# Memory keys and values beside the gate projections, and value stores issued by ScalarE

## The chip, the cores and the metric

The kernel runs on one core of one Trainium2 chip. The metric is the device time of one execution in microseconds. Its engines are TensorE (PE in the profile; its weight loads are PEld), VectorE (DVE), ScalarE (ACT), GpSimd (POOL) and SyncE (SP), which here issues DMAs and computes nothing. Each engine executes its own list of instructions in order; semaphores order the lists among each other.

## The reference

A network of three blocks on a sequence of 1024 rows of 1024 numbers, in float32. The change lies in layer A, the first of the last two:

```python
mem_n = rms_norm_2(mem, mem_norm)                      # 256 memory tokens
hn = rms_norm_2(h, norm_pre[i])
k_m, v_m = ...  (mem_n @ w_mem_kv[i])                  # for both layers, 4 heads of 64
c_q, c_kv, k_r, q_m, gate = split_cols(hn @ w_in_a[j], [384, 256, 32, 256, 1024])
main = mla_mixer(c_q, c_kv, k_r, positions, ...)       # 12 heads; 64 plain and 32 rotary columns
mem_out = memory_attention(q_m, k_m, v_m)              # every row reads all memory tokens
y = concatenate([main, mem_out]) * silu(gate)
h = h + rms_norm_2(y @ w_out[i], norm_post[i])
```

`mla_mixer` norms the latents `c_q` and `c_kv`, projects them to queries, keys and values, applies the rotary embedding to 32 columns of each query and to the shared `k_r`, and runs causal softmax attention. Layer B is alike with plain keys and values and a forget gate.

## The kernel before

Every matmul is done three times with operands split into a high and a low part (`mm3`, lines 124 to 126). A weight tile is loaded raw by `split_w` (line 103), rounded by ScalarE to its high part (`w_hi`, 104), and GpSimd subtracts for the low part (`w_lo`, 105).

The stages run one after another: start, stick, then mix, mlp and `layer_a` together, then `attn_a`, then `layer_b`. Within a stage a framework reorders each engine's instructions by its own estimate of when they can run, with the order in which the code emits them as its base; what comes out is fixed before the run. `merge(a, na, b, nb)` runs two generators by turns, `na` steps of the one beside `nb` of the other, so that they are emitted interleaved.

`layer_a` emits, in this order:
- `mem_norm`: the 256 memory tokens as two tiles of 128 rows are loaded (line 1090, one buffer for both), normed (lines 143 to 169, with a square root on ScalarE for which it loads a function table), transposed by TensorE (178) and split into `mh` and `ml`.
- 14 gate projections of 24 matmuls with 512 columns each (`gate`, PSUM tile `ps_ad`), evacuated by ScalarE with Silu, for which a table is loaded too (1205), and stored (1206).
- tables for the rotary embedding, the shared rotary key, the memory queries, the two latents and their norms.
- the rotary columns of the queries, in three groups `g` of four heads: six projections (`ps_r`), multiplied on VectorE (1274, 1277), summed on GpSimd (1278), split into `rope_hi` and `rope_lo` on ScalarE and VectorE (112, 113), and stored to `qrd` with four DMAs per group (1283), each with 16 rows of four heads (256 KB). `rope_hi` and `rope_lo` of group 2 reuse the buffers of group 0.
- `mem()` merged with `values()`. `mem` has eight projections of 24 matmuls with 256 columns (`ps_mem`): for each of two layers and two pairs of heads one for keys and one for values, with weights of 512 KB each, copies between partitions within SBUF (360), transposes of the values (370), and stores to DRAM (`mkv`, 1118, 1119). `values` has 16 units of six matmuls with 384 columns (`ps_v`), each evacuated by ScalarE into one of four buffers `vt_a` (1307) and stored to `vd_a` (1310; 192 KB in runs of 512 bytes).

`attn_a` reloads what was stored: rotary queries by lines 1353 and 1354, values by 1319, memory keys and values by `load_mkv` (1126, 1127). Its pools take the memory that `layer_a` gave back, so its first key evacuation (332) waits for the last value store. The method `values` also makes the values of layer B (`vd_b`, with a table of forget gates beside it).

All DMAs are issued on SP in one list. Each DMA raises one of eight counters, taken in turn, and waits until the DMA that had the same counter before it has landed.

Of the kernel before, what the change touches and what calls it, by code (L numbers as in the profile page):

```python
# [28 lines left out]
class Net:  # L29
# [1148 lines left out]
    def layer_a(self):  # L1178

        nc, tc, a = self.nc, self.tc, self.a  # L1180
# [8 lines left out]
        with ExitStack() as s2:  # L1189
            d1 = s2.enter_context(tc.tile_pool(name="ad1", bufs=1))  # L1190
            d2 = s2.enter_context(tc.tile_pool(name="ad2", bufs=2))
            psm = s2.enter_context(tc.tile_pool(name="psad", bufs=6, space=PSUM))
            pst = s2.enter_context(tc.tile_pool(name="pstad", bufs=2, space=PSUM))
# [3 lines left out]
            def unit(w, h):  # L1197
                ps = psm.tile([P, H], F32, name="ps_ad", tag="ad")
                self.proj_T(ps, w, col, act, 8, h)
                return ps  # L1200

            def gate(m, w, h):
                ps = unit(w, h)
                g = d2.tile([P, H], F32, name="g_ad", tag="kr1")
                nc.scalar.activation(out=g, in_=ps, func=AF.Silu)
                nc.sync.dma_start(out=gT[m, :, h * H:h * H + H], in_=g)

            self.mem_norm(d1, pst)
            for m in range(0, 8, 2):
                ws = [self.split_w(a["w_a_gate"][m + j], 1024) for j in range(2)] if m else self.g01  # L1210
                for h in range(0 if m else 1, 2):
                    for j in range(2):
                        gate(m + j, ws[j], h)
            cos = d1.tile([P, S], F32, name="cos")
            sin = d1.tile([P, S], F32, name="sin")
            rc = d1.tile([P, 3], F32, name="rope_c")
# [4 lines left out]
            w = self.split_w(a["w_a_kr"], 1024)  # L1221
# [12 lines left out]
            for p in range(2):  # L1234
                T = {k: d1.tile([P, S], F32R, name=f"qm_{k}", tag=f"qm_{k}") for k in ("qa", "qb")}
                w = self.split_w(a["w_a_qm"][p], 1024)
# [28 lines left out]
            for g in range(3):  # L1265
                w = self.split_w(a["w_mla_r"][g], 384)
# [19 lines left out]

            vt = d1.tile([P, 4, 384], F32, name="vt_a", tag="xq")

            def values():
                for n in range(2):  # L1290
                    w = [self.split_w(a["w_mla_v"][n], 768)]
                    yield from self.values(self.vd_a[3 * n:3 * n + 3], w, 2, range(3, 5), psm, "ad", vt)

            self.merge(self.mem(psm, pst, d2), 8, values(), 16)

    def values(self, vd, ws, kp, kts, psm, tag, vt, more=0, use=None):


        n = 384 + more
        hi, lo = self.act_hi, self.act_lo  # L1300
        for t in range(NT):
            ts = slice(t * P, (t + 1) * P)
            ps = psm.tile([P, n], F32, name="ps_v", tag=tag)
            self.mm3(ps, [((hi[:, k, ts], lo[:, k, ts]), tuple(w[:, (j % kp) * n:(j % kp) * n + n] for w in ws[j // kp]))
                          for j, k in enumerate(kts)])
            v = vt[:, t % 4]
            self.nc.scalar.activation(out=v, in_=ps[:, :384], func=AF.Copy)
            if more:
                use(t, ps[:, 384:])
            self.nc.sync.dma_start(out=vd[:, :, t, :].rearrange("q p c -> p q c"),  # L1310
                                   in_=v.rearrange("p (q c) -> p q c", c=P))
            yield

# [86 lines left out]
    def fox_gates(self, st):  # L1400
# [26 lines left out]
        def early(psm):  # L1427
            units.append(values(psm, 0))
            for _ in range(6):
                next(units[0])  # L1430
# [193 lines left out]
```

## Time and profile before

| | |
|---|---|
| median of three runs | 2968.9 us |
| runs | 2968.9, 2965.43, 2971.95 us |
| the profiled execution | 2973.59 us, span 2971.8 us |
| mean granted clock of TensorE | 0.972 |
| TensorE busy | 2774.5 us, 93% of the span |
| ScalarE busy | 1218.9 us, 41% |
| bytes moved by DMA | 311.14 MB, mean 105 GB/s |

Times in the rows below are microseconds from the start of the span. "Idle" in a row is the time for which the engine stood still ahead of the instruction, and the name behind the arrow is what it waited for. A granted clock of 1.00 is 2.4 GHz, 0.50 is 1.2 GHz.

### The profile page before, as it was taken

Reading aid. Unit: us, or ns where it says so; the run is one execution under the profiler, and the core shown is the slowest. Engines: PE = TensorE matmul, PEld = TensorE weight load, DVE = VectorE, ACT = ScalarE, POOL = GpSimd, SP = SyncE. Lnnn points to the kernel's source line nnn. Section 1 sums busy time; section 2 is a strip of 40 time slices with the busy share of each in tenths; the row PEclk is TensorE's granted clock in tenths of the full one; section 3 lists DMA queues with packets and bytes.
Section 4 is the critical chain, followed back from the end, with each engine's and each line's share of the span. In section 5 each row is a group of like instructions: output and inputs, shape, how many; then the busy total and the mean of one; then the engine's idle time right before and its main releaser. Section 6 shows DMA issues by size and latency. Waiting matters only on the chain. (4 is left out here: it accounts for less than half of the span.)

```text
span 2971.8 us, 37779 instructions
## 1 busy us (share of the span) xinstructions
PE 2774.5 (93%) x13490; PEld 2312.0 (78%) x13490; DVE 1692.0 (57%) x3201; ACT 1218.9 (41%) x2368; POOL 995.9 (34%) x823
## 2 busy tenths in 40 slices
PE   7999999998999998999989899689989999999988
PEld 5888778877878887888867689677768978778867
DVE  6320288845387665666587435287872426666643
ACT  5111266642442222121144423377763535555543
POOL 4221111113345442223255212332324344455442
PEclk9999999998999999999989899799999999999999
DMA  5111211127323335323123322632344232222162
GB/s 206 50 44 63 75 56 55 61 70 263 109 77 122 108 106 193 108 90 109 43 82 144 116 87 71 184 116 92 112 142 168 99 112 65 72 72 73 49 234 93
DMA packets 130644, 311.14 MB, mean 105 GB/s; under 512 B 14796, under 2 KB 34892, under 8 KB 130456
## 3 DMA queue, kind: packets, MB, share of 16 engines
q1 hardware_dynamic: 130456, 308.72, 31.0%
q8 instruction: 107, 1.75, 0.2%
q14 instruction: 81, 0.66, 0.1%
HBM read 213.33 MB, written 85.38 MB: 101 GB/s over the span
## 5 line engine op out<-in xcount | busy, mean ns | idle before, releaser
L105 POOL TENSOR_TENSOR w_lo<-w_raw,w_hi 128x1024 fp32r<-128x1024 f32 (+5 forms) x220 | 452.8, 2067 | 1057.8 <-ACT w_hi L104 1055.6
L104 ACT ACTIVATE w_hi<-w_raw 128x1024 fp32r<-128x1024 f32 (+5 forms) x220 | 192.5, 886 | 407.2 <-PE ps L125 90.7
L124 PE MATMUL ps_m<-act_hi,w_hi 128*128 128x512 f32 x716 | 289.8, 405 | 28.6 <-ACT w_hi L104 11.6
L125 PE MATMUL ps_m<-act_lo,w_hi 128*128 128x512 f32 x716 | 283.9, 397 | 0.0
L126 PE MATMUL ps_m<-act_hi,w_lo 128*128 128x512 f32 x716 | 282.4, 396 | 0.0
L113 DVE TENSOR_TENSOR pl<-tp_at,ph 128x512 fp32r<-128x512 f32 (+3 forms) x416 | 222.8, 560 | 85.9 <-ACT ph L112 83.8
L112 ACT ACTIVATE ph<-tp_at 128x512 fp32r<-128x512 f32 (+3 forms) x416 | 196.8, 500 | 106.2 <-PE tp_at L299 95.8
L1017 DVE TENSOR_TENSOR acc<-ps_d,acc 128x512 f32<-128x512 f32 x240 | 161.9, 687 | 109.7 <-PE ps_d L126 109.7
L299 PE MATMUL tp_at<-ident,p 128*128 128x128 f32 x1280 | 204.2, 275 | 16.1 <-DVE pl L113 5.7
L254 ACT ACTIVATE p<-p,mx 128x256 f32<-128x256 f32 (+7 forms) x256 | 180.3, 706 | 81.9 <-DVE mx L243 50.3
L124 PE MATMUL ps_d<-w_hi,act_hi 128*128 128x512 f32 x512 | 202.4, 395 | 7.7 <-ACT act_hi L112 7.7
L125 PE MATMUL ps_d<-w_lo,act_hi 128*128 128x512 f32 x512 | 202.0, 395 | 0.0
L126 PE MATMUL ps_d<-w_hi,act_lo 128*128 128x512 f32 x512 | 199.4, 392 | 0.0
L299 PEld LDWEIGHTS tp_at<-ident,p 128*128 128x128 f32 x1280 | 152.1, 140 | 48.5 <-DVE pl L113 9.1
L124 PEld LDWEIGHTS ps_m<-act_hi,w_hi 128*128 128x128 f32 x716 | 136.8, 191 | 64.8 <-ACT w_hi L104 12.7
L751 PE MATMUL r_o<-w_hi,act_hi 128*128 128x512 f32 x384 | 151.1, 403 | 20.5 <-DVE ga L687 7.9
L126 PEld LDWEIGHTS ps_m<-act_hi,w_lo 128*128 128x128 f32 x716 | 136.0, 190 | 28.6
L125 PEld LDWEIGHTS ps_m<-act_lo,w_hi 128*128 128x128 f32 x716 | 136.9, 191 | 25.9
L291 PE MATMUL o_ps<-ph,v 128*128 128x512 f32 (+3 forms) x400 | 145.5, 364 | 8.5 <-ACT ph L112 4.3
L753 PE MATMUL r_o<-w_hi,act_lo 128*128 128x512 f32 x384 | 151.7, 396 | 0.0
L752 PE MATMUL r_o<-w_lo,act_hi 128*128 128x512 f32 x384 | 151.3, 396 | 0.0
L292 PE MATMUL o_ps<-pl,v 128*128 128x512 f32 (+3 forms) x400 | 146.7, 374 | 0.4 <-DVE pl L113 0.2
(389 smaller groups left out, 6938.1 us busy)
## 6 DMA issues: line engine op xcount, KB each, us to landing
w_raw<-in_w_in SPq DMA_DIRECT2D x40, 512.0 KB, 3.4
w_raw<-in_w_up SPq DMA_DIRECT2D x32, 512.0 KB, 3.9
f_rows_up<-f_out SPq DMA_DIRECT2D x32, 512.0 KB, 5.4
w_raw<-in_w_down SPq DMA_DIRECT2D x32, 512.0 KB, 4.4
f_raw<-f_rows_up SPq DMA_DIRECT2D x32, 512.0 KB, 3.8
xd<-x_o SPq DMA_DIRECT2D x16, 512.0 KB, 2.7
w_raw<-in_w_out SPq DMA_DIRECT2D x16, 512.0 KB, 8.6
x_o<-xd SPq DMA_DIRECT2D x16, 512.0 KB, 4.8
```

The source lines that it names most:

```text
L104: nc.scalar.activation(out=hi[:, sl], in_=raw, func=AF.Copy)
L105: nc.gpsimd.tensor_tensor(out=lo[:, sl], in0=raw, in1=hi[:, sl].bitcast(F32), op=ALU.subtract)
L112: nc.scalar.activation(out=hi, in_=src, func=AF.Copy)
L113: nc.vector.tensor_tensor(out=lo, in0=src, in1=hi.bitcast(F32), op=ALU.subtract)
L124: nc.tensor.matmul(out, lhsT=sh, rhs=mh, start=(i == 0), stop=False)
L125: nc.tensor.matmul(out, lhsT=sh, rhs=ml, start=False, stop=False)
L126: nc.tensor.matmul(out, lhsT=sl, rhs=mh, start=False, stop=(i == n - 1))
L254: nc.scalar.activation(out=p[:, :nk], in_=p[:, :nk], func=AF.Exp, scale=-1.0, bias=mx[:, 0:1], accum_out=it["sum"][:, j:j + 1])
L299: nc.tensor.transpose(tp[:, j * P:(j + 1) * P], it["p"][j][:, k * P:(k + 1) * P], self.ident)
L752: nc.tensor.matmul(r, lhsT=a, rhs=wl, start=False, stop=False)
L753: nc.tensor.matmul(r, lhsT=b, rhs=wh, start=False, stop=(k == 7))
L1017: nc.vector.tensor_tensor(out=acc[:, t, sl], in0=ps, in1=acc[:, t, sl], op=ALU.add)
```

## The change

The eight steps of `mem()` are emitted beside the 14 gate projections, right after `mem_norm`, and `values` runs alone behind the rotary columns. The store of each unit of values is issued by ScalarE, in layer A and in layer B; its place in the rotation of counters is shared with the DMAs that stay on SP.

```diff
--- before.py
+++ after.py
@@ -1206,11 +1206,16 @@
                 nc.sync.dma_start(out=gT[m, :, h * H:h * H + H], in_=g)
 
             self.mem_norm(d1, pst)
-            for m in range(0, 8, 2):
-                ws = [self.split_w(a["w_a_gate"][m + j], 1024) for j in range(2)] if m else self.g01
-                for h in range(0 if m else 1, 2):
-                    for j in range(2):
-                        gate(m + j, ws[j], h)
+
+            def gates():
+                for m in range(0, 8, 2):
+                    ws = [self.split_w(a["w_a_gate"][m + j], 1024) for j in range(2)] if m else self.g01
+                    for h in range(0 if m else 1, 2):
+                        for j in range(2):
+                            gate(m + j, ws[j], h)
+                            yield
+
+            self.merge(gates(), 14, self.mem(psm, pst, d2), 8)
             cos = d1.tile([P, S], F32, name="cos")
             sin = d1.tile([P, S], F32, name="sin")
             rc = d1.tile([P, 3], F32, name="rope_c")
@@ -1286,12 +1291,10 @@
 
             vt = d1.tile([P, 4, 384], F32, name="vt_a", tag="xq")
 
-            def values():
-                for n in range(2):
-                    w = [self.split_w(a["w_mla_v"][n], 768)]
-                    yield from self.values(self.vd_a[3 * n:3 * n + 3], w, 2, range(3, 5), psm, "ad", vt)
-
-            self.merge(self.mem(psm, pst, d2), 8, values(), 16)
+            for n in range(2):
+                w = [self.split_w(a["w_mla_v"][n], 768)]
+                for _ in self.values(self.vd_a[3 * n:3 * n + 3], w, 2, range(3, 5), psm, "ad", vt):
+                    pass
 
     def values(self, vd, ws, kp, kts, psm, tag, vt, more=0, use=None):
 
@@ -1307,7 +1310,7 @@
             self.nc.scalar.activation(out=v, in_=ps[:, :384], func=AF.Copy)
             if more:
                 use(t, ps[:, 384:])
-            self.nc.sync.dma_start(out=vd[:, :, t, :].rearrange("q p c -> p q c"),
+            self.nc.scalar.dma_start(out=vd[:, :, t, :].rearrange("q p c -> p q c"),
                                    in_=v.rearrange("p (q c) -> p q c", c=P))
             yield
 
```

What follows is in lines of the changed kernel where they differ by a few: evacuation of values 1310, their store 1313, rope stores 1288, loads of rotary queries 1356 and 1357.

TensorE at the head of the gate stage, `ps_ad` being a gate and `tp<-ident,xn_m` the transposes of the normed memory tokens. Before:

```order
L126 MATMUL ps_ad<-act_hi,w_lo 128x512
L125 MATMUL ps_ad<-act_lo,w_hi 128x512
L126 MATMUL ps_ad<-act_hi,w_lo 128x512
L178 MATMUL tp<-ident,xn_m 128x128 x8
L124 MATMUL ps_ad<-act_hi,w_hi 128x512
L125 MATMUL ps_ad<-act_lo,w_hi 128x512
L126 MATMUL ps_ad<-act_hi,w_lo 128x512
```

and now:

```order
L124 MATMUL ps_ad<-act_hi,w_hi 128x512
L125 MATMUL ps_ad<-act_lo,w_hi 128x512
L126 MATMUL ps_ad<-act_hi,w_lo 128x512
L178 MATMUL tp<-ident,xn_m 128x128 x16
L124 MATMUL ps_mem<-mh,w_hi 128x256
L124 MATMUL ps_ad<-act_hi,w_hi 128x512
L125 MATMUL ps_ad<-act_lo,w_hi 128x512
L126 MATMUL ps_ad<-act_hi,w_lo 128x512
```

Before, 58 gate matmuls stand between the first of them and the first eight transposes, and 47 between those and the other eight. Now 24 stand ahead of the first, and the sixteen stand in one row with the first memory matmul behind them.

SP in the stage of the values, from the first rope store. Before:

```order
L1283 DMA qrd<-rope_hi 4x16x1024 x2
L1283 DMA qrd<-rope_lo 4x16x1024 x2
L360 DMA m_ka<-m_ka 64x256
L360 DMA m_kb<-m_kb 64x256
L1310 DMA vd_a<-vt_a 128x3x128 x2
L1118 DMA mkv<-m_ka 128x256
L1118 DMA mkv<-m_kb 128x256
L1118 DMA mkv<-m_kl 128x256
L103 DMA w_raw<-in_w_mla_v 128x768
L103 DMA w_raw<-in_w_mem_kv 128x1024
L1283 DMA qrd<-rope_hi 4x16x1024 x2
L1283 DMA qrd<-rope_lo 4x16x1024 x2
```

and now:

```order
L1288 DMA qrd<-rope_hi 4x16x1024 x2
L1288 DMA qrd<-rope_lo 4x16x1024 x2
L103 DMA w_raw<-in_w_mla_k 128x256
L103 DMA w_raw<-in_w_mla_q 128x384
L1357 DMA act_hi<-qrd 32x1024
L1356 DMA act_hi<-qrd 64x1024
L1288 DMA qrd<-rope_hi 4x16x1024 x2
L1288 DMA qrd<-rope_lo 4x16x1024 x2
L1356 DMA act_hi<-qrd 64x1024
L1357 DMA act_hi<-qrd 32x1024
L1288 DMA qrd<-rope_hi 4x16x1024 x2
L1288 DMA qrd<-rope_lo 4x16x1024 x2
```

The memory copies, stores and weights are gone from between the rope stores, the value stores are too, and the loads of rotary queries (`act_hi<-qrd`) have moved up between the groups of stores: the load with 64 rows, ahead of group 1, reads what all four stores of group 0 wrote.

ScalarE there. Before:

```order
L1307 ACTIVATE vt_a<-ps_v 128x384
L112 ACTIVATE rope_hi<-rope_14272 128x512
L1307 ACTIVATE vt_a<-ps_v 128x384
L366 ACTIVATE vt<-ps_mem 128x256
L112 ACTIVATE rope_hi<-rope_14290 128x512
L1307 ACTIVATE vt_a<-ps_v 128x384
L112 ACTIVATE rope_hi<-rope_14320 128x512
L1307 ACTIVATE vt_a<-ps_v 128x384
L104 ACTIVATE w_hi<-w_raw 128x768
```

and now:

```order
L1310 ACTIVATE vt_a<-ps_v 128x384
L1313 DMA vd_a<-vt_a 128x3x128
L112 ACTIVATE rope_hi<-rope_14631 128x512
L1310 ACTIVATE vt_a<-ps_v 128x384 x2
L104 ACTIVATE w_hi<-w_raw 128x256
L1313 DMA vd_a<-vt_a 128x3x128 x2
L112 ACTIVATE rope_hi<-rope_14661 128x512
L1310 ACTIVATE vt_a<-ps_v 128x384 x2
L104 ACTIVATE w_hi<-w_raw 128x384
L1310 ACTIVATE vt_a<-ps_v 128x384
L1313 DMA vd_a<-vt_a 128x3x128 x2
L112 ACTIVATE rope_hi<-rope_14679 128x512
```

Each evacuation is now followed, at once or after one or two other instructions, by the store of its buffer on the same engine. By the rotation of counters the fifth store waits for the second `rope_hi` store of group 0 to have landed, the tenth for one of `rope_hi` of group 1, the eleventh and twelfth for those of `rope_lo` of group 1, the fifteenth for the second `rope_hi` store of group 2, and the sixteenth for the first `rope_lo` store of group 2.

## Rows read from the trace of the kernel before

**Rows 1.** The page: its first line, and the first line of its part 1 (busy time of each engine, share of the span, instructions).

```profile
span 2971.8 us, 37779 instructions
...
PE 2774.5 (93%) x13490; PEld 2312.0 (78%) x13490; DVE 1692.0 (57%) x3201; ACT 1218.9 (41%) x2368; POOL 995.9 (34%) x823
```

**Rows 2.** Windows: the stretch, its length, busy time and instructions of TensorE (PE), its weight load, VectorE, ScalarE and GpSimd, then granted clock, DMA share and GB/s. Two of the seven windows of 20 us from 1700 to 1840, which all read 20.00 for TensorE.

```profile
1700.00:1720.00 20.00, 20.00 (x90) 16.57 (x89) 19.52 (x21) 4.64 (x6) 5.69 (x2) 1.00 0.32 113
...
1820.00:1840.00 20.00, 20.00 (x171) 20.00 (x171) 13.41 (x51) 8.81 (x33) 2.40 (x1) 1.00 0.14 47
```

**Rows 3.** Timeline of TensorE: start, length, engine, line, operation, what it writes and reads, count, and in brackets the idle time before it and who ended it, at the head of the gate stage. tp<-xn_m are the transposes of the memory tokens.

```profile
1662.96 0.96 PE L124 MATMUL ps_ad<-act_hi,w_hi 128*128 128x512 f32 x3 [0.69 <-ACT act_hi L112]
...
1681.98 1.94 PE L178 MATMUL tp<-ident,xn_m 128*128 128x128 f32 x8 [5.07 <-issue]
...
1696.12 1.04 PE L178 MATMUL tp<-ident,xn_m 128*128 128x128 f32 x8
```

**Rows 4.** The same view of ScalarE (ACT), VectorE (DVE) and SP there: the chain that normalises the two tiles of memory tokens.

```profile
1674.68 1.06 ACT L163 ACTIVATE xn_m<-m 128x1024 f32<-128x1024 f32 x1 [6.02 <-DMA rope_c<-in_rope_const]
...
1675.85 1.28 ACT L145 ACT_TABLE_LOAD   x1
...
1686.09 1.06 ACT L163 ACTIVATE xn_m<-m 128x1024 f32<-128x1024 f32 x1 [1.54 <-DMA m<-in_mem]
...
1678.48 3.40 DVE L169 SCALAR_TENSOR_TENSOR xn_m<-m,rstd_y,g_mem 128x1024 f32<-128x1024 f32 x1 [0.22 <-DVE rstd_y L149]
...
1691.39 1.28 DVE L169 SCALAR_TENSOR_TENSOR xn_m<-m,rstd_y,g_mem 128x1024 f32<-128x1024 f32 x1
...
1681.94 0.33 SPq L1090 DMA_DIRECT2D m<-in_mem  x1
```

**Rows 5.** Windows of that stretch, columns as in rows 2.

```profile
1682.00:1684.00 2.00, 2.00 (x9) 2.00 (x10) 0.27 (x1) 0.64 (x2) 0.00 (x0) 0.50 0.44 94
...
1688.00:1690.00 2.00, 2.00 (x11) 1.65 (x10) 0.00 (x0) 1.98 (x3) 1.49 (x1) 1.00 0.11 42
```

**Rows 6.** Timeline of TensorE in the stage of the values: the first and last of 17 memory matmuls (ps_mem, 256 columns) in a row.

```profile
1923.81 0.28 PE L125 MATMUL ps_mem<-ml,w_hi 128*128 128x256 f32 x1
...
1925.73 0.28 PE L126 MATMUL ps_mem<-mh,w_lo 128*128 128x256 f32 x1
```

**Rows 7.** Groups of instructions between 1855 and 1945: line, engine, operation, shapes, count | busy us, mean ns | idle time before them and who ended it.

```profile
L124 PE MATMUL ps_mem<-mh,w_hi 128*128 128x256 f32 x64 | 19.8, 309 | 22.0 <-ACT w_hi L104 16.9 <-ACT vt_a L1307 5.0
...
L1307 ACT ACTIVATE vt_a<-ps_v 128x384 f32<-128x384 f32 x16 | 7.6, 486 | 26.2 <-DMA vd_a<-vt_a 24.6 <-PE ps_v L126 1.5
```

**Rows 8.** Timeline of SP, the queue of all DMAs: issues of the rope stores (each row stands for two stores) and of the last value store. The length is that of the issue.

```profile
1858.42 1.23 SPq L1283 DMA_DIRECT2D qrd<-rope_hi  x2
1860.67 2.77 SPq L1283 DMA_DIRECT2D qrd<-rope_lo  x2
...
1876.91 1.15 SPq L1283 DMA_DIRECT2D qrd<-rope_hi  x2
...
1893.06 1.18 SPq L1283 DMA_DIRECT2D qrd<-rope_hi  x2
...
1928.96 0.41 SPq L1310 DMA_DIRECT2D vd_a<-vt_a  x1
```

**Rows 9.** Timelines of ScalarE and VectorE: the instructions there that waited for a rope store (qrd) or a value store (vd_a) to land.

```profile
1869.51 0.63 ACT L112 ACTIVATE rope_hi<-rope 128x512 fp32r<-128x512 f32 x1 [2.61 <-DMA qrd<-rope_hi]
...
1893.66 1.06 ACT L1307 ACTIVATE vt_a<-ps_v 128x384 f32<-128x384 f32 x2 [8.99 <-DMA vd_a<-vt_a]
...
1909.63 0.49 ACT L1307 ACTIVATE vt_a<-ps_v 128x384 f32<-128x384 f32 x1 [12.60 <-DMA vd_a<-vt_a]
...
1874.45 0.69 DVE L113 TENSOR_TENSOR rope_lo<-rope,rope_hi 128x512 fp32r<-128x512 f32 x1 [4.77 <-DMA qrd<-rope_lo]
```

**Rows 10.** Windows in the stage of the values, columns as in rows 2.

```profile
1862.00:1864.00 2.00, 2.00 (x18) 2.00 (x17) 1.91 (x5) 0.84 (x2) 2.00 (x1) 1.00 0.25 66
1880.00:1882.00 2.00, 0.75 (x3) 0.75 (x4) 1.31 (x4) 1.53 (x5) 2.00 (x2) 0.50 0.25 74
1898.00:1900.00 2.00, 0.00 (x0) 0.00 (x0) 0.00 (x0) 0.00 (x0) 0.00 (x0) 0.50 0.26 93
1920.00:1925.00 5.00, 5.00 (x42) 5.00 (x41) 1.18 (x4) 1.26 (x4) 0.12 (x1) 1.00 1.09 333
```

**Rows 11.** Timelines of ScalarE and TensorE at the end of that stage: the first key evacuation of the attention and its first score matmul.

```profile
1931.35 0.59 ACT L332 ACTIVATE ka<-ps_m 64x512 fp32r<-64x512 f32 x1 [0.33 <-DMA vd_a<-vt_a]
...
1942.19 0.41 PE L221 MATMUL s_ps<-act_hi 128*128 128x256 f32 x1
```

**Rows 12.** The line of the value stores, in layer A and in layer B: count, then shortest, median and longest issue in ns, first and last start; the last row is the time from issue to landing in layer B.

```profile
L1310 SPq DMA_DIRECT2D vd_a<-vt_a x16: 384/641/1992, 1866.8 to 1929.0; - x16
...
L1310 SPq DMA_DIRECT2D vd_b<-vt_b x15: 359/360/377, 2335.3 to 2395.6; - x15
...
DMA to landing us min/median/max: 2.0/2.3/2.7
```

**Rows 13.** A window of the values of layer B, columns as in rows 2.

```profile
2355.00:2375.00 20.00, 20.00 (x120) 19.76 (x119) 3.30 (x8) 9.38 (x16) 3.65 (x2) 1.00 0.16 49
```

## The prediction

> **What bounds the kernel now.** The page comes first: TensorE is busy for 93% of a span of 2971.8 us [rows 1], so a change pays only where TensorE waits, and costs wherever it adds work to a stretch in which TensorE never waits. Then I read the two stretches the change touches, in windows and in the timeline of each engine.
>
> Stretch A, the gate projections and what follows, is saturated: from 1700 to 1840 every window of 20 us shows TensorE busy for all 20.00 at a granted clock of 1.00 [rows 2]. One hole lies at its head. TensorE has 58 gate matmuls in front of the first transpose of the normalised memory tokens; they run from 1662.96 to about 1676.9, and the transpose waits until 1681.98 [rows 3] for a chain of one token tile: ScalarE's xn_m at 1674.68, a table load, VectorE's xn_m from 1678.48 for 3.40 us. The second tile's load is issued only at 1681.94, when that releases its buffer, and its xn_m starts on ScalarE at 1686.09 [rows 4]. That costs nothing today: 47 more gate matmuls stand between the two groups of transposes. After the hole TensorE runs at half clock (0.50, then 1.00 from 1688) [rows 5].
>
> Stretch B, from 1855 to 1942, holds the memory tokens' projections and the values, and TensorE waits there: 22.0 us before its ps_mem groups, while ScalarE's value evacuations wait 24.6 us for the stores of their four buffers [rows 7]. What ends B is the landing of the last value store: ScalarE's first key evacuation of the attention ends its wait on vd_a at 1931.35, and the first scores start at 1942.19 [rows 11]. Before it, three groups of rope stores pace everything (four stores of 256 KB each). The first group is issued from 1858.42 [rows 8]; its first pair has landed at 1869.51 and its second at 1874.45 [rows 9], so a group takes 16.0 us. The value stores behind group two end their wait at 1893.66, those behind group three at 1909.63 [rows 9], 16.8 and 16.6 us after the groups' first issues at 1876.91 and 1893.06 [rows 8]. A window in which almost nothing else moves shows a DMA share of 0.25 or 0.26 at 66 to 93 GB/s [rows 10]: a fraction of the engines, fully taken.
>
> **The change part by part.** I count by when events happen, against 2973.59 us of the profiled run, which is 4.7 above the median of 2968.9.
>
> 1. Memory projections into A. 192 matmuls, 0.12 us apart (16 steps from 1923.81 to 1925.73 [rows 6]), are 23.0 us; with the value transposes, 23.5. A has no idle TensorE time to take them [rows 2], so all of what follows is later by that.
>
> 2. The head of A. The order now puts 24 gate matmuls before the transposes instead of 58, and nothing between the two groups. At the 0.23 us a matmul of today (13.9 us for 58 [rows 3]) and with 0.6 for transposes among them they end at about 1669.1. The first tile is ready at 1681.98 as now, since its chain hangs on ScalarE's 1674.68 [rows 4]: 12.9 us idle. The second: load issued at 1681.94, xn_m at 1686.09 for 1.06; from the end of the first xn_m (1675.74) to VectorE's start are 2.74 us with a table load of 1.28 inside, 1.46 without it, as the load is gone; then 1.28 for the other xn_m [rows 4]: ready at 1689.9. TensorE ends the first eight transposes at 1683.9 (1.94 us [rows 3]): 6.0 idle. Together 18.9 against 5.07 today: +13.8, and about +1 because the second eight run at half clock (1.94 instead of 1.04 [rows 3]): +14.8. Bounds: 13, if VectorE's first xn_m takes 1.28 instead of 3.40 and wins half of that; 18, as the gate evacuation and the table load now stand ahead of rstd_t (0.6 + 1.28), and the weights' half-clock spell may repeat.
>
> Rope, stores and values thus start 38.3 us later. On SP the memory stores and copies now lie between gate loads; A's DMA share is 0.14 to 0.32 [rows 2], so I take nothing for them.
>
> 3. Stretch B without the memory tokens. Start is the first rope store (1858.42 before, 1896.7 after). By SP's order each loads-from-qrd now stands ahead of the next group's stores and waits for the group before it: group two cannot be issued until group one landed, 16.0 + 0.5. Group three's first pair is issued once group two's first pair landed, so it queues behind group two without a gap. For groups two and three I take 13.5 us, 1.05 MB at 78 GB/s, the mean of the three rows [rows 10]. The value stores now wait on ScalarE. Every DMA waits until the one eight earlier in its rotation has landed, and by the order of both queues the last two value stores come behind group three's first pair and its third store: three quarters of a group, 10.1 us. Then the last store, 2.3 us, what the same store takes in layer B where little else moves [rows 12]. Sum 16.0 + 0.5 + 13.5 + 10.1 + 2.3 = 42.4, against 72.9 today (1858.42 to 1931.35): 30.5 back. Bounds: at the best rate, 93 GB/s [rows 10], a group takes 11.3, and a first group of 14 gives 36.3; at the 16.7 of group two, with 3 us for the last store, 48.7. ScalarE has time for it: 16 evacuations of 0.49 [rows 7] and 16 issues of 0.64 [rows 12] are 18 us. Behind a waiting store stand the next evacuation and rope_hi of the next group; the order puts rope_hi of group two behind the fifth store, which waits for a pair that lands 11 us in, still before the 16.5. TensorE needs 17 us for the values and waits anyway.
>
> The Trainium skill speaks here: page "DMA: Bandwidth & Descriptors", section "Why a DMA increments its semaphore by 16 and not by 1", has a copy run on the largest number of engines, up to 16, that divides the slowest dimension of both sides, which for four heads by sixteen rows is four. The share of about 0.25 [rows 10] agrees. Its specifications give about 27 GiB/s for an engine, so four would take an estimated 9 us for a group; the sum for B by that is 27.6, not 42.4, and the rows, where no window at that share passes 93 GB/s, speak against it.
>
> 4. Values of layer B by ScalarE. 16 issues of 0.36 us [rows 12] are 5.8 us on an engine that is busy 9.4 of 20 us at most beside a saturated TensorE [rows 13]: nothing, and 5.8 if that cover were gone.
>
> The sum: 23.5 + 14.8 - 30.5 = **+7.8 us**, 2981.4 for the profiled run and 2976.7 for the median: 2977. With all bounds on one side: 23.0 + 13 - 36.6 = -0.6 and 24 + 18 - 24.2 = +17.8.
>
> **The rivals.** First, forecast: slower by 2 to 18, chance 0.60.
>
> Second, rope groups at the best rate seen, 93 GB/s: B takes 33.6 (11.3 + 0.5 + 11.3 + 8.5 + 2.0), net -1.0, 2968. For it: the queue no longer carries memory stores and weights. Against: group one took 16.0 with little beside it [rows 8, 9, 10]. Chance 0.22.
>
> Third, faster: the rope stores need less than 9.4 us a group when nothing shares the queue. To show as faster, B must come down by 38.3 + 5.9 from 72.9, to 28.7 us; less 0.5 and 2.3 that is 25.9 for two groups and three quarters. At 8.5 us a group B takes 8.5 + 0.5 + 8.5 + 6.4 + 2.3 = 26.2, net -8.4, 2960. The point from which it decides is 9.4 us a group, 112 GB/s. For it: the same core moves 333 GB/s in another window of B [rows 10], and layer B's value stores land in 2.0 to 2.7 us [rows 12]. Against it: no row at that share is near it. By the 9 us that the Trainium skill's page gives for four engines, above, B takes 27.6 and the result is 7.0 faster, on this side of the point. Chance 0.15.
>
> Fourth, slower by 20: the value stores on ScalarE hold up rope_hi of groups two and three, so that the groups no longer touch, and B takes 16.0 + 16.7 + 2 + 16.6 + 3 = 54.3: 2973.6 + 19.7, 2989 for the median. For it: ScalarE executes in order and waits in front of each store. Against: only the fifth and ninth store stand before such a step. Chance 0.03; it is the far end of the first.
>
> **How the numbers follow.** A change of this kernel shows from about 0.2%, 5.9 us; three runs spread over 6.5. The predicted time is the first case's, 2977; its own range is 2970 to 2987. The whole range reaches to the third case at 2960 and to just under the fourth: 2960 to 2988. Slower by over 0.2% is some five sixths of the first and the fourth: 0.53. Within it: the rest of the first and nearly all of the second: 0.31. Faster: the third and a little of the second: 0.16.
>
> **What would show it.** At the head of A: idle before the transposes of xn_m of about 12.9 and 6.0 us instead of 5.07. Between 1690 and 1890: ps_mem groups without idle time, and the first rope store near 1897. In B: ScalarE's issue of value stores waiting on DMA qrd, group two issued some 16.5 us after group one, group three landing some 40 us after the first store, the key evacuation ending its wait on vd_a near 1939 and the first scores near 1950. The prediction is wrong if the rope groups land in under 9.4 us each, if TensorE finds other work at the head of A, or if the end of B hangs on something the last value store does not hold.

## The result, and the profile after

The changed kernel takes 2987.57 us (median of four runs, 2983.82 to 2990.25) against 2967.16 for the kernel before (four runs, the three listed above and one more): the ratio, which is estimated apart from these medians, is 1.0075, with a 95% interval of 1.0058 to 1.0092. It is slower by 0.75%, as forecast; the forecast was 2977, 8 us slower, and it is 20 us slower. Nothing of the 20 us is more work; the page still gives TensorE the same busy time, over a longer span (compare [rows 1]):

```profile
span 2986.9 us, 37758 instructions
...
PE 2775.1 (93%) x13490; PEld 2311.6 (77%) x13490; DVE 1683.0 (56%) x3201; ACT 1216.5 (41%) x2366; POOL 993.8 (33%) x823
```

The span grew by 15.1 us between the two profiled executions; the profiled execution of before was 6.4 us above the median of its runs and that of the changed kernel 1.1 above its own, and the 5.3 between them is the rest. I count in the two traces, and come back to the scatter at the end.

At the head of the gate stage, the timeline of TensorE (compare [rows 3]):

```profile
1663.46 0.50 PE L124 MATMUL ps_ad<-act_hi,w_hi 128*128 128x512 f32 x1 [0.69 <-ACT act_hi L112]
...
1680.18 1.94 PE L178 MATMUL tp<-ident,xn_m 128*128 128x128 f32 x8 [10.49 <-issue]
1688.15 1.94 PE L178 MATMUL tp<-ident,xn_m 128*128 128x128 f32 x8 [6.03 <-DVE xn_m L169]
```

and the chain that normalises the memory tokens, on ScalarE, VectorE and SP (compare [rows 4]):

```profile
1673.57 1.06 ACT L163 ACTIVATE xn_m<-m 128x1024 f32<-128x1024 f32 x1 [8.54 <-DMA rope_c<-in_rope_const]
...
1684.38 1.06 ACT L163 ACTIVATE xn_m<-m 128x1024 f32<-128x1024 f32 x1 [1.62 <-DMA m<-in_mem]
...
1678.80 1.28 DVE L169 SCALAR_TENSOR_TENSOR xn_m<-m,rstd_y,g_mem 128x1024 f32<-128x1024 f32 x1 [0.21 <-DVE rstd_y L149]
...
1686.72 1.28 DVE L169 SCALAR_TENSOR_TENSOR xn_m<-m,rstd_y,g_mem 128x1024 f32<-128x1024 f32 x1
...
1680.11 0.33 SPq L1090 DMA_DIRECT2D m<-in_mem  x1
```

The first transposes wait 10.49 us and the second 6.03, instead of 5.07 in all, and both groups run at half clock (1.94 us each). VectorE's first xn_m took 1.28 us where it took 3.40 before, so the first tile was ready 1.8 us sooner than forecast.

Behind the head the stage is as saturated as it was, with the memory projections inside, while in the stage of the values TensorE now works for 1.34 of 20 us (windows; columns as in [rows 2]):

```profile
1720.00:1740.00 20.00, 20.00 (x102) 17.00 (x101) 1.43 (x4) 6.83 (x11) 9.42 (x4) 1.00 0.49 167
1800.00:1820.00 20.00, 20.00 (x90) 16.54 (x89) 6.31 (x8) 5.88 (x10) 3.34 (x2) 1.00 0.31 109
1920.00:1940.00 20.00, 1.34 (x6) 1.01 (x6) 1.24 (x3) 3.57 (x7) 0.00 (x0) 0.58 0.52 158
```

The stage of the values, from SP's list (compare [rows 8]; a row stands for two stores, or for one load of rotary queries, act_hi):

```profile
1895.01 1.25 SPq L1288 DMA_DIRECT2D qrd<-rope_hi  x2
...
1912.57 0.51 SPq L1356 DMA_DIRECT2D act_hi<-qrd  x1
1913.14 1.11 SPq L1288 DMA_DIRECT2D qrd<-rope_hi  x2
...
1925.99 0.32 SPq L1357 DMA_DIRECT2D act_hi<-qrd  x1
1926.42 5.11 SPq L1288 DMA_DIRECT2D qrd<-rope_hi  x2
1934.71 2.00 SPq L1288 DMA_DIRECT2D qrd<-rope_lo  x2
```

what SP waited for there (us in total, times, longest):

```profile
SPq L1357 <- DMA vd_a<-vt_a: 15.3, 4, 5.5
...
SPq L1288 <- DMA vd_a<-vt_a: 7.8, 3, 3.8
```

and its end, on ScalarE and TensorE (compare [rows 11]; the first row is the issue of the last value store):

```profile
1942.04 0.37 ACTq L1313 DMA_DIRECT2D vd_a<-vt_a  x1
1950.00 0.59 ACT L332 ACTIVATE ka<-ps_m 64x512 fp32r<-64x512 f32 x1 [9.29 <-DMA act_lo<-qrd]
...
1960.16 0.42 PE L221 MATMUL s_ps<-act_hi 128*128 128x256 f32 x1
```

The value stores themselves, in layer A and then in layer B: issue in ns (shortest, median, longest), first and last start, and time to landing (compare [rows 12]):

```profile
L1313 ACTq DMA_DIRECT2D vd_a<-vt_a x16: 366/392/2772, 1889.5 to 1942.0; - x16
...
DMA to landing us min/median/max: 8.1/11.6/15.4
...
L1313 ACTq DMA_DIRECT2D vd_b<-vt_b x16: 366/366/381, 2357.0 to 2420.8; - x16
...
DMA to landing us min/median/max: 2.0/2.0/3.1
```

From the first rope store the three groups are issued at 0, +18.1 and +31.4 us, the last pair of the third at +39.7, the last value store at +47.0, and it lets the key evacuation go at +55.0. Before, that took 72.9. The bracket of the evacuation names a load of rotary queries instead, because a few steps of that load's counter came last; the evacuation waits for the counter of the last value store too, and the trace has the sixteenth and last step of that one at 1949.78, 7.7 us after the issue.

The landing rows cover only the stores whose landing the profile could tell, 6 of 16 in layer A here. The trace also holds every step of the eight counters, and a DMA's steps lie between its issue and the next issue on its counter. Counted so, all sixteen stores of layer A land in 2.4 to 15.4 us, median 10.2; the 2.4 is the first store, which goes out ahead of the first rope store, and the others take 7.1 or more. Before, it was 2.3 to 12.2, median 5.2. In layer B the same engine's queue lands the same store in 2.0 us in the median.

Between anchors of the traces, then:

| us | before | after |
|---|---|---|
| first gate matmul | 1662.96 | 1663.46 |
| to the first rope store | 195.5 | 231.5 |
| to the first key evacuation | 72.9 | 55.0 |
| to the first score | 10.8 | 10.2 |
| to the end of the span | 1029.6 | 1026.7 |

### The profile page after: what moved, and what is told of

Its sections match the earlier page's. It is cut to its first block, busy times and chain, and to the rows that moved or that the text cites. A ratio compares the mean times of both kernels' runs of the same rounds, so it can differ in the third digit from the quotient of the medians.

```text
span 2986.9 us, 37758 instructions
## 1 busy us (share of the span) xinstructions
PE 2775.1 (93%) x13490; PEld 2311.6 (77%) x13490; DVE 1683.0 (56%) x3201; ACT 1216.5 (41%) x2366; POOL 993.8 (33%) x823
## 5 line engine op out<-in xcount | busy, mean ns | idle before, releaser
L124 PE MATMUL ps_m<-act_hi,w_hi 128*128 128x512 f32 x716 | 290.2, 405 | 47.6 <-issue 17.5
```

The source lines that it names most:

```text
L124: nc.tensor.matmul(out, lhsT=sh, rhs=mh, start=(i == 0), stop=False)
```

## The experiments

"First rope store to first score" is called the stretch; it was 83.8 us before and 65.2 after. All times are medians, beside runs of the kernel before on the same chip (their medians are 2966.8 to 2968.9). "All sixteen" marks a landing time counted from the steps of the counters, as above.

**One part at a time.** First the memory projections alone:

```diff
-            self.nc.scalar.dma_start(out=vd[:, :, t, :].rearrange("q p c -> p q c"),
+            self.nc.sync.dma_start(out=vd[:, :, t, :].rearrange("q p c -> p q c"),
```

> The changed kernel with the value stores issued on SP again; TensorE's order is that of the changed kernel. Theory 1 (in the changed kernel a value store of 512-byte runs in a queue of its own takes turns with the 4 KB runs of the rope stores on the four engines these use, which is why it lands after 8.1 to 15.4 us): back behind the rope stores in one queue the median landing falls to 8 us or less, and the time to 2975 to 2983. Theory 2 (the queue does not matter, the groups of rope stores alone pace the stretch): within 4 us of the changed kernel's 2987.6. Page's rule of the skill that issuing elsewhere saves the issue time only: 16 issues of 0.4 to 2 us go back to SP, up to 5 us slower.

Measured: 2983.1, ratio to before 1.0040 (1.0027 to 1.0053). SP's issue of the last rope pair, the landing of the value stores, the first key evacuation and the first score:

```profile
1927.14 2.86 SPq L1288 DMA_DIRECT2D qrd<-rope_lo  x2
...
DMA to landing us min/median/max: 4.5/8.9/9.7
...
1946.64 0.59 ACT L332 ACTIVATE ka<-ps_m 64x512 fp32r<-64x512 f32 x1 [4.91 <-DMA act_lo<-qrd]
...
1954.72 0.28 PE L221 MATMUL s_ps<-act_hi 128*128 128x256 f32 x1
```

Then the stores alone, the same line changed the other way in the kernel before:

> The kernel before with the value stores issued by ScalarE and the memory projections left beside the values; the head of the gate stage is as before (58 and 47 gate matmuls around the transposes). Theory 1 (turns with the rope stores' runs): median landing above 10 us instead of 7.7, first score no earlier than 1942, time 2967 to 2975. Theory 2: within 4 us of 2967.2. If the issue by ScalarE is what helps and the memory projections are what hurts: under 2961.

Measured: 2967.6, ratio 0.9999 (0.9984 to 1.0014). The first rope store, the landing, the first score:

```profile
1855.03 1.23 SPq L1283 DMA_DIRECT2D qrd<-rope_hi  x2
...
DMA to landing us min/median/max: 2.7/7.0/13.0
...
1935.67 0.28 PE L221 MATMUL s_ps<-act_hi 128*128 128x256 f32 x1
```

So the memory projections beside the gates alone cost 16 us by the medians and 12 by the ratio, and the issue by ScalarE costs nothing alone and something on top of them: 4.5 us by the medians, 10 by the ratios, whose intervals just miss each other, and 5.7 us of the stretch. In mem_only SP waits for no value store, the last rope pair goes out 31.9 us after the first store (1927.14) and not 39.7, and the stretch is 59.5 us. The last value store is issued hardly earlier, at +46.5 (1941.76), but it lands in 4.5 us instead of 7.7: by the counters the last rope store had landed at 1940.0 there, and in the changed kernel only at 1946.3. (The bracket of the evacuation names a load here too; the counter of the last value store ends at 1946.27.) The run fits neither theory's numbers: 2983.1 us and a median landing of 8.9 (all sixteen: 8.6) lie at the edge of theory 1, 4.5 us is just beyond theory 2, and the third guess had the wrong sign. Theory 1 does not come out of act_only well: in a queue of their own beside the memory projections the value stores landed in 7.0 us in the median, no later than the 7.7 of before (all sixteen: 4.8 and 5.2).

**The head of the gate stage.**

```diff
-            self.merge(gates(), 14, self.mem(psm, pst, d2), 8)
+            gs = gates()
+            for _ in range(4):
+                next(gs)
+            self.merge(gs, 10, self.mem(psm, pst, d2), 8)
```

> The changed kernel with four gate projections emitted ahead of the first step of the memory projections. Its order again has 58 gate matmuls before the first eight transposes of the memory tokens and 47 before the other eight. Theory (the head of the gate stage costs 11 to 12 us because 34 gate matmuls no longer cover the norm of the memory tokens): idle there 5 us instead of 10.5 + 6.0, first rope store near 1884 instead of 1895, time 2974 to 2978. Rival (the idle time only moves, since the chain of the second token tile then delays the first memory projections, and weights come late): 2984 or more.

Measured: 2974.6, ratio 1.0019 (1.0006 to 1.0033). TensorE at the head, with GpSimd's w_lo and VectorE's first xn_m beside it, and the first rope store:

```profile
1667.24 0.96 PE L124 MATMUL ps_ad<-act_hi,w_hi 128*128 128x512 f32 x3 [0.69 <-ACT act_hi L112]
...
1681.68 2.92 POOL L105 TENSOR_TENSOR w_lo<-w_raw,w_hi 128x1024 fp32r<-128x1024 f32 x1 [21.55 <-ACT w_hi L104]
...
1681.07 1.28 DVE L169 SCALAR_TENSOR_TENSOR xn_m<-m,rstd_y,g_mem 128x1024 f32<-128x1024 f32 x1 [0.21 <-DVE rstd_y L149]
...
1682.46 1.06 PE L178 MATMUL tp<-ident,xn_m 128*128 128x128 f32 x8 [1.27 <-issue]
...
1694.05 1.04 PE L178 MATMUL tp<-ident,xn_m 128*128 128x128 f32 x8
...
1882.10 1.25 SPq L1291 DMA_DIRECT2D qrd<-rope_hi  x2
```

With 58 gate matmuls ahead of them again, the first transposes wait 1.27 us and run at full clock, and the second eight do not wait. That took 13 of the 20 us back by the medians, 17 by the ratios. This trace makes the head look better than it need be: VectorE's first xn_m took 1.28 us in it, and in the run pieces_head below, with the same head, it took 3.40 and the wait is 4.24 us. There GpSimd's w_lo had started just ahead of it; the section on the prediction comes back to it.

**The rope stores.** A store takes 64 partitions to four heads of 16 rows. In the run spread these 64 rows lie next to each other in DRAM, and the loads pick up what belongs to a head:

```diff
-        qrd = self.qrd = self.dram.tile([12, 64, S], F32, name="qrd")
+        qrd = self.qrd = self.dram.tile([3, 4, 64, S], F32, name="qrd")
...
-                        nc.sync.dma_start(out=qrd[4 * g:4 * g + 4, r:r + 16, :], in_=x[64 * b:64 * b + 64].bitcast(F32))
+                        nc.sync.dma_start(out=qrd[g, 2 * j + b], in_=x[64 * b:64 * b + 64].bitcast(F32))
...
-                        nc.sync.dma_start(out=qr[x][0:64].bitcast(F32), in_=self.qrd[2 * p + x])
-                        nc.sync.dma_start(out=qr[x][64:96].bitcast(F32), in_=self.qrd[2 * p + x, 0:32])
+                        g, q = divmod(2 * p + x, 4)
+                        nc.sync.dma_start(out=qr[x][0:64].bitcast(F32), in_=self.qrd[g, :, 16 * q:16 * q + 16])
+                        nc.sync.dma_start(out=qr[x][64:96].bitcast(F32), in_=self.qrd[g, 0:2, 16 * q:16 * q + 16])
```

> The changed kernel with another layout of the rotary queries in DRAM: the 64 rows that a rope store writes lie next to each other, so both of its sides have 64 as slowest dimension; the loads of rotary queries now read four pieces of 16 rows. Theory (rope stores use four of sixteen DMA engines and everything else in the stretch queues there): DMA share over 0.5 while rope stores run, a group of four lands in 5 to 7 us instead of 16, value stores in 3 to 5 us, the stretch from the first rope store to the first score falls from 65 to 35 to 45 us, time 2957 to 2967. Rival (64 partitions of SBUF, or DRAM, set the rate, not the number of engines): groups still take over 12 us, time within 5 us of 2987.6.

Measured: 2974.4, ratio 1.0024 (1.0008 to 1.0040). The three groups, a window, the first score, and the longest new wait behind it:

```profile
1895.43 1.11 SPq L1288 DMA_DIRECT2D qrd<-rope_hi  x2
...
1905.52 1.14 SPq L1288 DMA_DIRECT2D qrd<-rope_hi  x2
...
1915.81 1.35 SPq L1288 DMA_DIRECT2D qrd<-rope_hi  x2
...
1901.00:1903.00 2.00, 2.00 (x14) 2.00 (x13) 1.94 (x4) 1.30 (x3) 1.16 (x1) 1.00 0.98 274
...
1938.70 0.28 PE L221 MATMUL s_ps<-act_hi 128*128 128x256 f32 x1
...
PE s_ps L221 <- DMA v_raw<-vd_a: 7.3, 1, 7.3
```

Groups are issued 10 us apart, the DMA share is 0.98 where it was 0.25 [rows 10], the value stores land in 6.0 us in the median (all sixteen; 10.2 in the changed kernel), and the stretch is 43.3 us instead of 65.2. Nothing but the place of the rows in DRAM was changed, with the same bytes and as many DMAs, so the four engines were what paced the groups. The counters say the same: the trace of the changed kernel has one step of a rope store's counter at its issue and four after it, and that of spread has sixteen. From its first issue to its last landing a group took 17.5 to 19.9 us there and 9.3 to 11.5 here. The theory had 5 to 7 us for a group and 2957 to 2967 for the time, and both were missed. Of the 21.9 us, 13 remain in the time: the loads of rotary queries now have four or two pieces on one side, their counters take one step and then four or two, and a load of values behind them keeps the scores waiting for 7.3 us.

**Shorter or longer runs.** What was left of theory 1 was tested in the changed kernel with value rows of 384 numbers:

```diff
-        self.vd_a = self.dram.tile([6, P, NT, P], F32, name="vd_a")
+        self.vd_a = self.dram.tile([2, P, NT, 384], F32, name="vd_a")
...
-            self.nc.scalar.dma_start(out=vd[:, :, t, :].rearrange("q p c -> p q c"),
-                                   in_=v.rearrange("p (q c) -> p q c", c=P))
+            self.nc.scalar.dma_start(out=vd[:, t, :], in_=v)
```

> The changed kernel with the values stored in DRAM as rows of 384 numbers: the store of a unit writes runs of 1536 bytes instead of 512, the same bytes; the loads of values read runs of 512 bytes. Theory (on the four engines of the rope stores a value store gets one packet for one packet of 4 KB, so the number of its packets sets when it lands): median landing falls from 11.6 us to 5 to 7, SP's waits on value stores from 23 us to under 12, the stretch from the first rope store to the first score from 65 to 55 to 60 us, time 2978 to 2983. Rival (the bytes ahead on those engines set it): landing over 9 us, time within 4 us of 2987.6.

Measured: 2989.9, ratio 1.0074 (1.0051 to 1.0097). The landing, the last rope pair, the first score:

```profile
DMA to landing us min/median/max: 7.2/9.3/11.1
...
1930.25 2.33 SPq L1288 DMA_DIRECT2D qrd<-rope_lo  x2
...
1957.64 0.41 PE L221 MATMUL s_ps<-act_hi 128*128 128x256 f32 x1
```

Landing went from 11.6 to 9.3 us (all sixteen: 10.2 to 8.6) and not to 5 to 7; the last rope pair leaves 38.3 us after the first (1891.93), the stretch is 65.7, the time is that of the changed kernel. Theory 1 falls: a third of the runs took only a sixth off the landing. What is left, and fits all these runs, is that value stores and rope stores share the four engines, and that by the rotation each list waits for stores of the other. No run changed the rotation alone, so its share is read from the waits and not shown by an experiment.

**The same on the kernel before, and both together.** spread_before is the kernel before with the layout of spread; in pieces_before each head is loaded in six pieces of 16 rows:

```diff
-                        nc.sync.dma_start(out=qr[x][0:64].bitcast(F32), in_=self.qrd[g, :, 16 * q:16 * q + 16])
-                        nc.sync.dma_start(out=qr[x][64:96].bitcast(F32), in_=self.qrd[g, 0:2, 16 * q:16 * q + 16])
+                        for r in range(6):
+                            nc.sync.dma_start(out=qr[x][16 * r:16 * r + 16].bitcast(F32), in_=self.qrd[g, r % 4, 16 * q:16 * q + 16])
```

> The kernel before with the rows of a rope store next to each other in DRAM, as in the run spread. Theory (rope stores on four engines pace the stretch of the values there too, and the memory projections only fill TensorE's waits): first rope store to first score falls from 83.8 us to 55 to 65, of which some 7 are given back by loads of rotary queries on four engines, time 2945 to 2955. Rival (memory weights, copies and stores in SP's single list pace it): over 75 us, time 2959 to 2968.

> As spread_before, and each load of rotary queries in pieces of 16 rows, six DMAs for a head instead of two, so that its sides are both 16 rows. Theory (in the run spread the first scores were followed by a wait of 7.3 us for a load of values that stood behind loads of rotary queries on four engines): that wait is gone, 5 to 8 us faster than spread_before. Rival (three times as many DMAs in SP's list and in the rotation of counters cost as much): not faster than spread_before.

Measured: 2955.0, ratio 0.9956 (0.9942 to 0.9971), and 2948.7, ratio 0.9928 (0.9906 to 0.9951). The stretch is 73.3 us in the one and 60.5 in the other. In the first that is more than the theory's 55 to 65 and less than the rival's 75, with the time at the upper end of the theory's range; the second shows that 12.8 us of it belonged to loads on few engines, and a share of SP's list in the rest is not shown. Pieces are 6 us faster by the medians, in spite of their number; the two intervals overlap. pieces_before, the first rope store, the landing, the first score:

```profile
1854.66 1.12 SPq L1283 DMA_DIRECT2D qrd<-rope_hi  x2
...
DMA to landing us min/median/max: 2.1/2.7/4.8
...
1915.17 0.41 PE L221 MATMUL s_ps<-act_hi 128*128 128x256 f32 x1
```

pieces_head is the changed kernel with the edits of head, spread and pieces:

> The changed kernel with the three edits: four gate projections ahead of the memory projections, rope stores to neighbouring rows, loads of rotary queries in pieces of 16 rows. If the parts add up: 2987.6, less 13 for the head, less 21.5 for the stretch of the values, is 2953, and below the kernel before. If the 8 us that the run spread gave back behind the first score are not due to the loads: 2960. Against pieces_before it tells whether the memory projections are worth more beside the gates or beside the values once the rope stores no longer pace: beside the values they cost what TensorE lacks there, beside the gates 19 to 24 us.

Measured: 2949.6, ratio 0.9938 (0.9917 to 0.9959).

```profile
1677.66 2.34 POOL L105 TENSOR_TENSOR w_lo<-w_raw,w_hi 128x1024 fp32r<-128x1024 f32 x1 [21.81 <-ACT w_hi L104]
...
1677.68 3.40 DVE L169 SCALAR_TENSOR_TENSOR xn_m<-m,rstd_y,g_mem 128x1024 f32<-128x1024 f32 x1 [0.21 <-DVE rstd_y L149]
...
1681.19 1.94 PE L178 MATMUL tp<-ident,xn_m 128*128 128x128 f32 x8 [4.24 <-issue]
...
1880.46 1.11 SPq L1291 DMA_DIRECT2D qrd<-rope_hi  x2
...
1918.30 0.28 PE L221 MATMUL s_ps<-act_hi 128*128 128x256 f32 x1
```

The first rope store comes 217.5 us after the first gate matmul against 195.7 in pieces_before, 21.8 later; the stretch is 37.8 against 60.5, 22.7 shorter. The parts nearly add up (2953 was worked out), and the two places of the memory projections come out alike.

**The issue and the place once more, with spread rope stores.**

> The run pieces_head with the value stores issued on SP again. Theory (the issue by ScalarE cost 4 to 6 us in the changed kernel because SP's rope stores and value stores waited for each other by the rotation while both were slow on four engines): with the rope stores on all engines the place of issue is worth nothing, 2946 to 2953. Rival (a second list as such delays SP): 4 to 6 us faster than pieces_head, 2944 or less.

> The run pieces_before with the value stores issued by ScalarE, the memory projections beside the values. Theory: within 4 us of 2948.7. If SP's list, which here also carries the memory stores, is what still holds the stretch (70.1 us from the first rope store to the first score): under 2944.

> The run pieces_before with the first layer's four steps of the memory projections beside the gates (after four gate projections) and the other four beside the values. Theory (beside the gates each of the two halves costs 11.5 us of TensorE; beside the values it costs what TensorE lacks there): first rope store 11 us later than in pieces_before, the stretch to the first score 11 to 15 us shorter than 70.1, so 2944 to 2950: no place is worth more than the other once the rope stores are spread. If the second half fits into TensorE's waits beside the values, where 44 us without any memory projection still hold some 15 us of waits: under 2943.

Measured: 2946.2 (ratio 0.9925, 0.9908 to 0.9941), 2949.1 (0.9931, 0.9906 to 0.9956) and 2949.9 (0.9936, 0.9913 to 0.9959). All five kernels with pieces lie between 2946 and 2950, and their intervals overlap: with the rope stores on all engines neither the engine that issues the value stores nor the place of the memory projections shows in the time. pieces_head_sp is 3.4 us faster than pieces_head, which is not clear of the noise, and its stretch is the same, 37.8 us in both.

pieces_half has 214.1 us to the first rope store and a stretch of 43.7. (The 70.1 us that two of the expectations give for the stretch of pieces_before does not stand in its trace, which has 60.5.) That is 18.4 us later and 16.8 shorter than in pieces_before. The two nearly cancel, as the theory had it, but they are not the half that it worked out, 11 us: 96 memory matmuls at 0.12 us are 11.5, and on top of them come ten matmuls of the values, a wait for ScalarE and a slower clock behind it (0.65, then 0.93, from 1724 to 1732):

```profile
1724.13 0.44 PE L370 MATMUL tp_v<-ident,vt 128*128 128x128 f32 x2 [3.31 <-ACT vt L366]
```

**A second trace of before.**

> The kernel before once more, for a second trace: its profiled execution was 6 us above the median of its runs. If that lies ahead of the changed stretches: first gate matmul near 1659 instead of 1662.96, with 195 us to the first rope store and 83 to 84 from there to the first score as before. If it lies in the stretch of the values: 78 to 81 us there, as in act_only's 80.6.

Measured: 2974.2 beside 2968.0. Gates began at 1659.98, the first rope store came 195.9 us later, the first score 82.5 after that, and the rest took 1034.1 where it had taken 1029.6. Neither guess was right: the stretches that the change touches repeat within 1.3 us, and the scatter is spread over what lies ahead and behind.

## Why the prediction was wrong

Its direction held, and so did what it said of the memory projections and of the head. The median lies just inside its whole range (2960 to 2988) and just outside that of the forecast case (2970 to 2987). The size did not hold: 20 us and not 8, by the stage of the values. Point by point, in the traces:

- *The memory projections in a saturated stage, 23.5 us.* Held, a little smaller: from the first gate matmul to the first rope store pieces_head takes 21.8 us more than pieces_before, with the head nearly equal. The sum had counted all 192 matmuls, but in the trace of before 24 of them already ran ahead of the first rope store; eight matmuls of the values run there now: 168 at 0.12 us and eight at 0.17 are 21.5.
- *The head, +14.8.* Held in kind, a little below its lower bound of 13: the trace has 11.5 us more waiting at the transposes and 0.9 for the second transposes at half clock, and the undoing of it (head) took 13 us back. Both parts together were forecast as 38.3 and measured as 36.1 (231.5 less 195.5, less rounding). The term that I gave 3.40 us, VectorE's first xn_m, took 1.28. Before, GpSimd's w_lo had started 0.02 us ahead of it; now it had ended, at 1678.1. No run set out to try this, but the fourteen traces agree: xn_m took 3.40 us in the seven in which w_lo had started 0.02 us ahead of it, and 1.28 or 1.29 in the seven others. Half of this was in my lower bound.
- *The stage of the values, 42.4 us to the first key evacuation.* **This step failed**: it took 55.0, outside its bounds of 36.3 to 48.7. The first half was good: group two was issued at +18.1 (forecast 16.5), the first pair of group three at +31.4. Two terms were wrong. First, "it queues behind group two without a gap", and with it the 10.1 us from there to the last value store, which measured 15.6. I counted when the first pair of group three could be issued and not the rest of the group: by the rotation the second store of that pair waits until the eighth value store has landed, and the second pair until the ninth and tenth have. The ninth and tenth landed after 12.7 and 12.9 us, so the second pair went out 8.3 us behind the first and the last value store 6.9 us later than worked out (47.0 against 40.1). SP waited 23.1 us for value stores by the rows above, 17.4 of it ahead of that pair. Second, the last store's 2.3 us, taken from layer B as the nearest row: it let go after 8.0. The row was the wrong one not for its layer but because no rope store was in flight there. The last store of before took 2.3 us too (issued at 1928.96 [rows 8], the evacuation behind it started at 1931.35 [rows 11]), 20 us after the last rope store had landed, and stores beside rope stores took up to 12.2 us in the same stretch. The prediction itself had put the last value store right behind the rope stores, on the four engines that it had found fully taken. 6.9 + 5.7 = 12.6 is the whole miss of the step.
- *The rivals.* The fourth, chance 0.03, gave B 54.3 us and the median 2989; measured were 55.0 and 2987.6. Its mechanism was half right: the third group was stretched, since the lists wait for each other, but it was SP that waited for value stores; ScalarE's wait in front of the fifth store ended at 1906.82, well ahead of the second group. I gave it too little because I looked for waits of ScalarE on SP's stores alone, where the rotation works both ways.
- *Four engines.* By the rule of the Trainium skill, page "DMA: Bandwidth & Descriptors", section "Why a DMA increments its semaphore by 16 and not by 1", a rope store runs on four engines; the share of 0.25 said so, and spread shows it: with 64 as slowest dimension on both sides the share is 0.98. The estimate of 9 us for a group, from the figure for an engine in that page's section "Specifications", was not reached in any kernel with four engines: from first issue to last landing their groups took 14.1 to 21.7 us. In spread the same rule turned against the loads, whose sides then had a slowest dimension of four, and six pieces of 16 rows cured it.
- *ScalarE as issuer, nothing.* Right for layer B (landing 2.0 us) and alone (act_only), wrong by 4.5 us or more in the combination. The prediction weighed the issue time and ScalarE's own waits, and not that one list on SP kept the order in which rope and value stores were issued: with it SP waited for no value store and the last group had landed 1.8 us before the last value store went out (mem_only).

From the anchors the account of the 15.1 us is: +0.5 ahead of the gates, +36.1 to the first rope store, -17.9 to the key evacuation, -0.7 to the score, -2.9 behind it, where only the issuer of layer B's value stores differs.

## What to carry to other kernels

Before work is moved out of a stretch of waits, ask what paces the waits: here it was not the work moved but the stores of the rotary queries, on four of sixteen DMA engines, and with their 64 rows next to each other and loads in pieces the kernel was 17 to 21 us faster than before, wherever the memory projections stood. A producer that is moved up needs the cover it had: 34 matmuls fewer ahead of a norm, and none left between its two tiles, cost 13 us. When DMAs of two lists share one rotation of counters, follow the waits in both directions, and price a transfer by a row with the same other transfers in flight. When a profile gives a landing time, ask how many of the transfers it covers.

## What the runs showed of the hardware that was not expected

A store of 192 KB lands in 2.0 us or in 15.4 depending on what else uses the four engines, in the same queue, and tripling its runs to 1536 bytes changed its median only from 10.2 to 8.6 us (all sixteen). The steps of a DMA's counter in the trace tell on how many engines it ran: five records for a rope store of four heads by 16 rows, sixteen for one of 64 rows in a row, five or three for the loads of spread. VectorE's xn_m of 128 x 1024 took 3.40 us where GpSimd's w_lo had started 0.02 us ahead of it and 1.28 elsewhere; where w_lo started inside xn_m, it was w_lo that took longer, 2.9 to 3.1 us instead of 2.34. And one and the same code ahead of the change reached the first gate matmul anywhere between 1658.9 and 1667.2 us in fourteen traces, and the code behind the first score took 1026.7 to 1034.1 in the six traces that differ there in nothing but the issuer of layer B's value stores: differences of a few us between single traces say nothing. Stretches between near anchors repeat better. With the old order of the gates the first rope store came 193.9 to 195.9 us after the first gate matmul in five traces; in a sixth (pieces_before_act), whose xn_m took 1.28 us, it came after 189.3.
